# Loading the first two batches of b one by one, and entering the block through GpSimd, in a batched A^T B^T matmul

## The chip, the cores and the metric

The kernel runs on one core of a Trainium2 chip. The metric is device microseconds of one execution. The profile covers one execution; its span (123.0 us before) is about 2 us shorter than the time outside it (124.96 us).

## The reference

```python
batch, m, k, n = 16, 512, 512, 512
a: [batch, k, m] float32      b: [batch, n, k] float32
reference = np.matmul(a.transpose(0, 2, 1), b.transpose(0, 2, 1))   # [batch, m, n] float32
```

33.55 MB are read and 16.78 MB written, 50.33 MB in all. a is stored with k first and is used as it is; b is transposed on the chip.

## The kernel before

Every load and the last stores are issued by SP; the other stores by ScalarE. b comes in pairs of batches: a partition holds 8 rows of 2 KB, 16 KB that lie together in memory, and the loads move them in 16 KB packets. VectorE casts a pair to bf16 in two halves, TensorE transposes it through an identity (`turn`), VectorE copies the PSUM result to SBUF once for each batch, and TensorE multiplies (`half`). The pair is transposed as a whole: batch 0's copy can start only after both halves are transposed.

```python
b_v = b.rearrange("(p g) (ni r) k -> p (g ni) r k", g=2, r=NR)      # NR = 8
...
with tc.tile_critical():                       # entered through SP
    ...
    def run_sp(sp):
        for i in range(B):
            for p in ([0] if i == 0 else [(i + 1) // 2] if i % 2 and i + 1 < B else []):
                if p >= PAIRS:
                    sp.wait_ge(turned, p - PAIRS + 1)
                sp.dma_start(b_sb[p % PAIRS][:], b_v[p]).then_inc(b_in[p % PAIRS], 16)
            s, use = i % LOADS, i // LOADS     # LOADS = 4
            if use:
                sp.wait_ge(summed, MO * (i - LOADS) + 1)
            if i % 2 == 0 and i // 2 >= OUTS:
                sp.wait_ge(o_out[i // 2 % OUTS], 16 * (i // 2 // OUTS))
            sp.dma_start(a_sb[s][:], a_v[i]).then_inc(a_in[s], 16)
        ...                                    # the last three pairs of outputs are stored here
    def run_act(act):
        cast_a(act, 0)
        for i in range(B - 1):
            cast_a(act, i + 1)
            copy_out(act, i, slice(2, 4), oa_go)
            j, odd = divmod(i - LAG, 2)        # LAG = 3
            if odd and 0 <= j < H - TAIL:
                store(act, j)
        ...
```

## Time and profile before

| | before |
|---|---|
| time, median of the first 3 runs | 124.96 us (124.85 to 125.09) |
| span of the profiled execution | 123.0 us |
| DMA queues, share of the 16 engines' span | 77.2% + 20.1% |
| rate of the DMA engines from 6 to 118 us | 425 to 430 GB/s |
| TensorE, VectorE, ScalarE busy | 70%, 46%, 38% |

The packets of the two queues fill 97% of the 16 DMA engines' span. The lines behind the table, and what follows from them, are in the prediction.

### The profile page before, as it was taken

The numbers are of one execution on the slowest core, as the hardware profiler recorded it, in microseconds if no ns is written. First come the engines' busy times: TensorE is split into PE (matmuls) and PEld (weight loads), VectorE is DVE, ScalarE is ACT, GpSimd is POOL, SyncE is SP. The second block draws the span as 40 slices with busy tenths as digits, with TensorE's granted clock in tenths as the row PEclk, the third lists the DMA queues.
The fourth block names the chain that finished last, engine by engine and source line by source line (L and its number), as shares of the span: only waits on it lengthen the run. The fifth ranks groups of instructions, "written<-read, shape, count | busy, mean of one in ns | idle before, by whom it ended". The sixth has DMA issues, their size and how long they took to land. (4 is left out here: it accounts for less than half of the span.)

```text
span 123.0 us, 1086 instructions
## 1 busy us (share of the span) xinstructions
PE 86.1 (70%) x400; PEld 49.7 (40%) x400; DVE 56.4 (46%) x48; ACT 46.8 (38%) x34; POOL 0.7 (1%) x6
## 2 busy tenths in 40 slices
PE   0006497997999799779930799965992679979600
PEld 0006344642755464346410546442640526437300
DVE  0016368478295755917039107780719306171200
ACT  4003209537717903176300950329230490750300
POOL 2000000000000000000000000000000000000000
PEclk9999999999999999999995557999999558999995
DMA  4999999999999999999999999999999999999992
GB/s 91 394 400 458 400 424 456 429 394 456 426 397 448 434 376 432 426 440 440 416 421 429 458 408 418 429 426 437 453 397 432 426 426 426 429 426 426 429 424 115
DMA packets 5648, 50.33 MB, mean 409 GB/s; under 512 B 528, under 2 KB 528, under 8 KB 528
## 3 DMA queue, kind: packets, MB, share of 16 engines
q1 hardware_dynamic: 4288, 39.85, 77.2%
q10 hardware_dynamic: 1360, 10.49, 20.1%
HBM read 33.55 MB, written 16.78 MB: 409 GB/s over the span
## 5 line engine op out<-in xcount | busy, mean ns | idle before, releaser
L219 PE MATMUL o_ps<-bt_sb,a_bf 128*128 128x512 bf16 x256 | 65.1, 403 | 7.1 <-PEq L194 6.6
L135 ACT CAST a_bf<-a_sb 128x2048 bf16<-128x2048 f32 x16 | 30.4, 1900 | 40.8 <-DMA a_sb<-in_a_dram 40.8
L219 PEld LDWEIGHTS o_ps<-bt_sb,a_bf 128*128 128x128 bf16 x256 | 28.5, 115 | 37.5 <-issue 15.0
L205 PE MATMUL bt_ps<-identity,b_bf 128*128 128x128 f32 x144 | 24.3, 323 | 22.7 <-PEq L194 22.7
L144 DVE COPY o_sb<-o_ps 128x1024 f32<-128x1024 f32 x16 | 19.6, 1224 | 35.8 <-PE o_ps L219 35.8
L205 PEld LDWEIGHTS bt_ps<-identity,b_bf 128*128 128x128 f32 x144 | 22.2, 212 | 28.2 <-issue 27.2
L152 DVE CAST b_bf<-b_sb 128x2048 bf16<-128x2048 f32 x16 | 19.5, 1221 | 19.1 <-DMA b_sb<-in_b_dram 19.1
L144 ACT COPY o_sb<-o_ps 128x1024 f32<-128x1024 f32 (+1 forms) x17 | 16.4, 962 | 28.0 <-PE o_ps L219 28.0
L161 DVE COPY bt_sb<-bt_ps 128x1024 f32<-128x1024 f32 x16 | 19.5, 1216 | 3.1 <-PE bt_ps L205 3.1
L135 ACT ACT_TABLE_LOAD x1 | 1.3, 1283 | 0.9 <-SPq L51 0.9
L122 POOL TENSOR_SCALAR_AFFINE_SELECT identity<-identity 128x128 f32<-128x128 f32 x1 | 0.3, 294 | 0.2 <-POOL identity L120 0.2
L120 POOL MEMSET identity<- 128x128 f32 x1 | 0.2, 205 | 0.7 <-SPq L51 0.7
L265 POOL MEMSET const-bfloat16-1.0<- 128x1 bf16 x1 | 0.1, 102 | 0.0
L265 POOL MEMSET const-uint8-127<- 128x1 uint8 x1 | 0.1, 102 | 0.0
L265 POOL MEMSET const-float32-0.0<- 128x1 f32 x1 | 0.1, 99 | 0.2 <-issue 0.2
L265 POOL MEMSET const-float32-1.0<- 128x1 f32 x1 | 0.1, 99 | 0.0
## 6 DMA issues: line engine op xcount, KB each, us to landing
b_sb<-in_b_dram SPq DMA_DIRECT2D x8, 2048.0 KB, 20.4
a_sb<-in_a_dram SPq DMA_DIRECT2D x16, 1024.0 KB, 17.5
out_dram<-o_sb ACTq DMA_DIRECT2D x5, 2048.0 KB, 15.2
out_dram<-o_sb SPq DMA_DIRECT2D x2, 2048.0 KB, 13.6
out_dram<-o_sb SPq DMA_DIRECT2D x2, 1024.0 KB, 6.3
```

What stands on the lines that cost most here:

```text
L120: pool.memset(identity[:], 0.0).then_inc(id_go, 1)
L122: pool.affine_select(out=identity[:], in_=identity[:], compare_op=mybir.AluOpType.not_equal, fill=1.0, base=0, pattern=[[-1, P]], channel_ ...
L135: act.copy(a_bf[i % 2][:], a_sb[s][:]).then_inc(ac_go, 1)
L144: copy(o_sb[i // 2 % OUTS][:, i % 2, rm, :], o_ps[h][:, p, :]).then_inc(go, 1)
L152: dve.tensor_copy(b_bf[:, r, :], b_sb[p % PAIRS][:, r, :]).then_inc(bc_go, n)
L161: dve.tensor_copy(bt_sb[g][:].rearrange("p j (ni r) -> p j ni r", r=NR), bt_ps[:].rearrange("p j r (g ni) -> p g j ni r", g=2)[:, g],).the ...
L205: last = pe.transpose(bt_ps[:, j, r, :], w[:, r, j, :], identity[:])
L219: last = pe.matmul(o_ps[h][:, q, :], a_r[:, rk, 2 * h + q, :], bt_h[:, rk // 2, rk % 2, :], start=(rk == 0), stop=(rk == KO - 1),)
L265: nc = _bacc.Bacc("TRN2", target_bir_lowering=False, num_devices=1)
```

## The change

The intent is an earlier start of computing. The first pair of b is loaded as two single batches, each in 8 KB packets, so that batch 0 can be cast and transposed while batch 1 is on its way; its PSUM copy no longer waits for batch 1. Later pairs stay as they were. The entry of the block is coordinated by GpSimd instead of SP, so that SP can issue sooner.

```diff
+    b0_v = b[0:2].rearrange("g (ni no) k -> g ni no k", no=NR // 2)
-    with tc.tile_critical():
+    with tc.tile_critical(sync_engine=nc.gpsimd.engine):
         def run_sp(sp):
+            for g in range(2):
+                sp.dma_start(
+                    b_sb[0][:, g * NR // 2:(g + 1) * NR // 2, :], b0_v[g]
+                ).then_inc((b_first, b_in[0])[g], 16)
             for i in range(B):
-                for p in ([0] if i == 0 else [(i + 1) // 2] if i % 2 and i + 1 < B else []):
+                for p in [(i + 1) // 2] if i % 2 and i + 1 < B else []:
... in run_dve, cast_b(0, 0) waits for b_first; turn(0, 0) waits for turned_first and copies in two parts:
+                if p == 0:
+                    r = NR // 2
+                    bt = bt_ps[:, :, g * r:(g + 1) * r, :].rearrange("p j r ni -> p j ni r")
... in run_pe, the first half's transposes are announced by themselves:
-                if h:
-                    last.then_inc(turned, 1)
+                if h or first:
+                    last.then_inc(turned if h else turned_first, 1)
```

## The prediction

> **What bounds the kernel now.** I read the page's slices first, then the rate in small stretches, then the waits, then the two ends of the timeline. The slices settle most of it:
>
> ```profile
> PE   0006497997999799779930799965992679979600
> DMA  4999999999999999999999999999999999999992
> DMA packets 5648, 50.33 MB, mean 409 GB/s; under 512 B 528, under 2 KB 528, under 8 KB 528
> ```
>
> The DMA row is 9 in every slice but the first and the last. No compute engine is like that: TensorE has idle slices until the end, and ScalarE and VectorE are each busy less than half of the span. The rate in stretches (columns: stretch, its length, busy time of PE, PEld, DVE, ACT, POOL, granted clock, DMA share, GB/s) says how full "9" is:
>
> ```profile
> 1.50:2.00 0.50, 0.00 (x0) 0.00 (x0) 0.00 (x0) 0.50 (x1) 0.29 (x1) 1.00 0.54 131
> 2.00:2.50 0.50, 0.00 (x0) 0.00 (x0) 0.00 (x0) 0.18 (x1) 0.00 (x0) 1.00 1.47 262
> 2.50:3.00 0.50, 0.00 (x0) 0.00 (x0) 0.00 (x0) 0.00 (x0) 0.00 (x0) 1.00 0.65 164
> 3.00:3.50 0.50, 0.00 (x0) 0.00 (x0) 0.00 (x0) 0.00 (x0) 0.00 (x0) 1.00 0.46 131
> ...
> 6.00:30.00 24.00, 17.00 (x80) 10.55 (x80) 13.78 (x12) 9.01 (x6) 0.00 (x0) 1.00 1.01 428
> 30.00:60.00 30.00, 26.37 (x134) 15.57 (x135) 17.91 (x16) 15.60 (x12) 0.00 (x0) 1.00 1.01 425
> 60.00:90.00 30.00, 21.86 (x96) 12.18 (x93) 14.15 (x12) 10.96 (x8) 0.00 (x0) 0.83 1.01 430
> 90.00:118.00 28.00, 20.89 (x94) 11.43 (x92) 10.56 (x9) 9.93 (x9) 0.00 (x0) 0.88 1.00 425
> 118.00:120.50 2.50, 0.00 (x0) 0.00 (x0) 0.00 (x0) 0.00 (x0) 0.00 (x0) 0.79 1.01 426
> 120.50:121.00 0.50, 0.00 (x0) 0.00 (x0) 0.00 (x0) 0.00 (x0) 0.00 (x0) 0.50 0.40 164
> ```
>
> From 6 to 120.5 us the 16 engines move 425 to 430 GB/s with a share of 1.0, in the stretch that only reads (6 to 30) as in the one that only writes (118 to 120.5). There is no hole in which a faster compute chain would let a transfer start sooner. The span can therefore be written as a sum along the DMA engines. The packet records in the trace (not a view of the page) give 309 ns (median) for an 8 KB packet and 611 ns for a 16 KB one. An engine carries a sixteenth of the 2048 a packets and the 2048 out packets of 8 KB, and of the 1024 b packets of 16 KB: 256 x 0.309 + 64 x 0.611 = 79.1 + 39.1 = 118.2 us; its 33 small semaphore packets of 9 ns add 0.3. In front stand 0.95 us until the first load is issued and 1.0 us until its first packet starts (1.96). The first packets are slow, 0.9 to 1.9 us instead of 0.61; summed over those that start before 3.4 us and divided by 16 this costs about 0.75 us. That makes 1.96 + 118.5 + 0.75 = 121.2; the last packet ends at 121.45, on one engine that lags the others. Its landing is seen at 121.93, and the waiting for `stored` and the closing barrier make 123.0. The timed median of 124.96 has about 2 us more than the span, outside the profile (the profiled execution itself took 124.78). So some 118.5 us of 125 are bytes, and what a change that leaves the bytes alone can touch is the 6.5 us at the ends.
>
> The waits (who waited <- for whom: total us, times, longest us) look as if there were more to win:
>
> ```profile
> ACT a_bf L135 <- DMA a_sb<-in_a_dram: 40.8, 9, 9.1
> DVE o_sb L144 <- PE o_ps L219: 35.8, 14, 6.3
> DVE b_bf L152 <- DMA b_sb<-in_b_dram: 19.1, 6, 8.8
> PE bt_ps L205 <- PEq L194: 22.7, 9, 10.2
> ```
>
> The compute engines wait for loads, and the longest wait of VectorE, 8.8 us, is the one at the start that the change attacks. But these are waits of engines that are not the bound. The beginning of the timeline (start us, duration us) has the chain that the change shortens, and the end has what follows the last load:
>
> ```profile
> 8.81 2.36 DVE L152 CAST b_bf<-b_sb 128x2048 bf16<-128x2048 f32 x2 [8.81 <-DMA b_sb<-in_b_dram]
> 10.18 3.61 PE L205 MATMUL bt_ps<-identity,b_bf 128*128 128x128 f32 x16 [10.18 <-PEq L194]
> 11.25 1.90 ACT L135 CAST a_bf<-a_sb 128x2048 bf16<-128x2048 f32 x1 [9.06 <-DMA a_sb<-in_a_dram]
> 13.83 1.23 DVE L161 COPY bt_sb<-bt_ps 128x1024 f32<-128x1024 f32 x1 [2.66 <-PE bt_ps L205]
> 15.55 3.80 PE L219 MATMUL o_ps<-bt_sb,a_bf 128*128 128x512 bf16 x16 [1.76 <-PEq L194]
> ...
> 92.23 24.65 SPq L86 DMA_DIRECT2D out_dram<-o_sb x4
> ```
>
> The last store is issued until 116.88, starting about 116.54. Its 1.05 MB are the last that move. At 426 GB/s they need 2.46 us, and they end about 120.8, so they start about 118.3; with the 1.0 us from issue to first packet seen at the start they could have started at 117.5. The compute tail therefore has a margin of some 0.8 us (estimate from these numbers): finishing earlier gains nothing, finishing more than 0.8 us later would open a hole.
>
> **What the Trainium skill says.** "DMA: Bandwidth & Descriptors", section "Bandwidth", gives 425 GB/s for a 16 MB load and 435 as the fabric ceiling of the 16 engines; the trace agrees with 425 to 430. The same page, "Issuing engines are not separate DMA queues", says that DMAs share the same 16 engines whoever starts them, and that issuing elsewhere saves sequencer time only; here two queues with 77.2% and 20.1% of the engines' span add to 97%, so the trace agrees. "TensorE: Matmul & The Clock Gate", "Part 1: The HAM clock gate", says that TensorE is clocked at half until it has been busy for some microseconds, and again after an idle window, and that the phase of that window varies. The trace has the clock at 0.5 in two stretches (about 65 to 75 and 96 to 102 us). That is the one thing that could move the tail.
>
> **The change part by part.**
>
> *Entry through GpSimd.* The gathering instruction at the entry of the critical block moves from SP to GpSimd. In the trace SP leaves the opening barrier at 0.67, runs its NOP at 0.72, passes its own semaphore at 0.80 and issues at 0.95. Now SP waits for a semaphore from GpSimd, which released the opening barrier itself at 0.61 and whose instructions there follow each other every 0.08 us: its NOP would be at about 0.69, SP would pass about 0.72 to 0.75. Gain on the path: some 0.05 us. At the exit the block's gathering also moves to GpSimd, but SP sits 4.6 us waiting for the last store there; nothing.
>
> *The first pair in two loads.* Same 2.10 MB, now 256 packets of 8 KB instead of 128 of 16 KB: per engine 16 x 309 = 4.94 us for 8 x 611 = 4.89, +0.06 us with one more semaphore packet, all on the DMA path. One more issue on SP of about 0.43 us moves every later issue back by that, but the first load keeps the engines busy for 2.5 us, so none of it shows. The slow first packets: if the slowness is a time, nothing changes; if it is a cost per packet, smaller packets change it by a few tenths either way. I take 0 with 0.3 of doubt.
>
> *Compute start.* Batch 0 of b lands about 2.5 us sooner (half the bytes at 427 GB/s): near 6.2 instead of 8.8. Its cast ends at 7.5, its 8 transposes at 9.3, while the second half lands at 8.8, is cast until 10.0 and turned until about 11.9. The PSUM copy, now in two parts of some 0.62 us (estimate: half of 1.23), runs 10.0 to 11.3 instead of 13.83 to 15.06. Then a0 becomes what the first matmul waits for: it lands at 11.2 as before, because it follows the same bytes in the queue, and its cast ends at 13.2. The first matmul thus starts near 13.2 instead of 15.55: 2.3 us sooner. This gain does not reach the end. The cast of a3 at 28.51 waited for its landing, so at batch 3 the gain falls to some 1.3 us, and a cast near 97 us again waited 6.6 us for a load whose issue depends on earlier stores landing. All of that is scheduling inside a DMA stream that is full anyway.
>
> Sum: 124.96 - 0.05 + 0.06 + 0 = about 124.95; I put 124.9.
>
> **The rivals.** (1) The earlier start is kept to the end and the time falls by up to 2.3 us, to 122.7. For it: the first matmul really moves, and waits of 40.8 and 19.1 us for loads look large. Against it: the DMA share is 1.0 from 3.5 to 120.5 us, so 50.33 MB would have to move at 436 GB/s, which no long stretch shows. I give it 1 in 100 for 2%. (2) The start-up of the DMA engines is what changes: smaller first packets fill the engines sooner and recover part of the 0.75 us, time about 124.3; or 8 KB packets each pay the slow start and the time is about 125.3. The low rate between 2.5 and 3.5 us speaks for something to win; that no packet record says why it is low, against. (3) The tail comes out of step: since compute runs 1 to 2 us ahead, stores enter the engines earlier and the last loads land a little later in the stream, or the half-clock stretch falls on the last batches. The slow stretch before 102 us had 8 matmuls in 3.48 us where 1.83 is usual, so 1.65 us; less the 0.8 of margin this costs about 1 us, 126. For it: the margin is thin. Against it: compute is ahead, not behind.
>
> **Range and chances.** Sources of doubt: start-up 0.3 us, the lagging engine at the end 0.3, run-to-run spread 0.1, the tail 1 us at a chance of 1 in 8, upward only. That gives 124.2 to 125.7. For 2% the time would have to fall to 122.5, or rise to 127.5; the first needs more than all that stands outside the bytes and the fixed ends, the second a hole of 2.5 us. Faster 1%, within 97%, slower 2%.
>
> **What would show it.** Right: the DMA share stays at 1.0 and 425 to 430 GB/s from about 4 to 120 us; the first cast of b begins near 6.2 and the first matmul near 13.2, its last wait being the cast of a; the first issue on SP is at about 0.90; the span is 122.6 to 123.6. Wrong: a stretch before 120 us with a share well under 1 (the tail); a sum of the first 3.5 us that differs clearly from 0.34 MB (the start-up); or a steady rate other than 427, which I take to be fixed and on which the whole prediction rests.

## The result, and the profile after

125.08 us (median of 6 runs, 124.92 to 125.30) against 124.97 for the kernel before in the same rounds (6 runs). The ratio is 1.0013, 95% interval 1.0000 to 1.0027: the same within 2%. Ratios here and below are the mean time of one kernel's runs over that of the other's of the same rounds, so they are not quite the ratio of the medians.

The slices of the changed kernel's page:

```profile
DMA  3999999999999999999999999999999999999992
DMA packets 5792, 50.33 MB, mean 409 GB/s; under 512 B 544, under 2 KB 544, under 8 KB 544
```

Its compute waits (total us, times, longest us):

```profile
ACT a_bf L143 <- DMA a_sb<-in_a_dram: 39.2, 9, 8.5
DVE o_sb L152 <- PE o_ps L239: 38.9, 13, 6.4
DVE b_bf L163 <- DMA b_sb<-in_b_dram: 19.3, 8, 5.8
PE bt_ps L225 <- PEq L214: 17.4, 10, 7.1
```

The DMA row is full from the second slice to the last but one, as before. VectorE's longest wait for b fell from 8.8 to 5.8 us, which is the head start the change wanted, and yet its total wait for b is 19.3 us where it was 19.1: what is not waited for at the start is waited for later.

The beginning of the changed kernel's timeline (start us, duration us):

```profile
0.89 0.86 SPq L97 DMA_DIRECT2D b_sb<-in_b_dram  x2
...
5.75 1.23 DVE L163 CAST b_bf<-b_sb 128x2048 bf16<-128x2048 f32 x1 [5.75 <-DMA b_sb<-in_b_dram]
...
10.70 1.90 ACT L143 CAST a_bf<-a_sb 128x2048 bf16<-128x2048 f32 x1 [8.53 <-DMA a_sb<-in_a_dram]
...
12.94 5.12 PE L239 MATMUL o_ps<-bt_sb,a_bf 128*128 128x512 bf16 x16 [1.39 <-PEq L214]
```

SP issues at 0.89 instead of 0.95; the first cast of b starts at 5.75 instead of 8.81; the first matmul at 12.94 instead of 15.55, held only by the cast of a0. But its 16 matmuls take 5.12 us where the same 16 took 3.80, so 2.6 us of head start are 1.3 by the end of batch 0 (18.06 against 19.35).

For the rate, the same stretches of both kernels (columns as in the prediction; the last two are DMA share and GB/s; a packet counts where it starts). Before:

```profile
3.00:6.00 3.00, 0.00 (x0) 0.00 (x0) 0.00 (x0) 0.00 (x0) 0.00 (x0) 1.00 0.88 360
42.00:46.00 4.00, 4.00 (x25) 2.72 (x24) 1.78 (x3) 1.28 (x1) 0.00 (x0) 1.00 0.97 397
118.00:118.50 0.50, 0.00 (x0) 0.00 (x0) 0.00 (x0) 0.00 (x0) 0.00 (x0) 1.00 1.02 426
```

After:

```profile
3.00:6.00 3.00, 0.00 (x0) 0.00 (x0) 0.25 (x1) 0.00 (x0) 0.00 (x0) 1.00 1.03 431
42.00:46.00 4.00, 4.00 (x23) 2.44 (x21) 2.36 (x2) 0.45 (x1) 0.00 (x0) 1.00 1.00 373
118.00:118.50 0.50, 0.00 (x0) 0.00 (x0) 0.00 (x0) 0.00 (x0) 0.00 (x0) 1.00 0.94 393
```

These lines show where the gain goes. The changed kernel is at full rate from 3 us, where the kernel before is at 360 GB/s. Between 42 and 46 us it loses: the share stays at 1.00 while the rate falls to 373 GB/s, so the engines are not idle; their packets take longer. (All of the slow ones are loads; the store packets take their steady 309 ns.) At 118 us there is a small hole.

Counted from the trace's packet records (each packet's bytes spread over its duration), this is how far the stream had come, in MB:

| by | before | after | after minus before |
|---|---|---|---|
| 6 us | 1.253 | 1.384 | +0.131 (0.31 us at 427 GB/s) |
| 42 us | 16.630 | 16.743 | +0.113 |
| 48 us | 19.133 | 19.105 | -0.028 |
| 116 us | 48.249 | 48.229 | -0.020 |

The change puts the stream 0.3 us ahead, keeps that for 36 us, and gives all of it back within 6 us, when the first stores enter (first store packet at 44.04 us before, 43.23 after). Two measures of slow packets are used from here on. *Start cost* is the sum, over the packets that start before 5 us, of duration less the steady duration of that packet size (611 ns for 16 KB, 309 for 8 KB, 159 for 4 KB), divided by 16: us per engine. *First-store cost* is the same for 40 to 50 us.

| | start cost | first-store cost |
|---|---|---|
| before | 0.80 | 0.18 |
| after | 0.57 | 0.51 |

The start cost differs from one execution to the next: in after, shift_half, shift_all and shift_ports, whose first 25 us are the same program, it is 0.57, 0.30, 0.63 and 0.32. Their position at 6 us is steadier (1.370 to 1.384 MB; 1.230 to 1.280 in the four traces that start with a 16 KB load of b), so the gain is better read from that.

### The profile page after: what moved, and what is told of

The parts are those of the page before. It is cut to its first block, busy times and chain, and to the rows that moved or that the text cites. A ratio compares the mean times of both kernels' runs of the same rounds, so it can differ in the third digit from the quotient of the medians.

```text
span 123.1 us, 1090 instructions
## 1 busy us (share of the span) xinstructions
PE 89.7 (73%) x400; PEld 49.7 (40%) x400; DVE 56.6 (46%) x49; ACT 46.7 (38%) x34; POOL 0.7 (1%) x6
## 5 line engine op out<-in xcount | busy, mean ns | idle before, releaser
L239 PE MATMUL o_ps<-bt_sb,a_bf 128*128 128x512 bf16 x256 | 69.2, 422 | 9.7 <-PEq L214 9.2
L239 PEld LDWEIGHTS o_ps<-bt_sb,a_bf 128*128 128x128 bf16 x256 | 29.2, 118 | 42.9 <-issue 22.7
L225 PEld LDWEIGHTS bt_ps<-identity,b_bf 128*128 128x128 f32 x144 | 21.5, 211 | 23.7 <-issue 22.9
L163 DVE CAST b_bf<-b_sb 128x2048 bf16<-128x2048 f32 x16 | 19.6, 1223 | 19.3 <-DMA b_sb<-in_b_dram 19.3
L181 DVE COPY bt_sb<-bt_ps 128x1024 f32<-128x1024 f32 (+1 forms) x17 | 19.5, 1153 | 0.5 <-PE bt_ps L225 0.5
```

The source lines that it names most:

```text
L163: dve.tensor_copy(b_bf[:, r, :], b_sb[p % PAIRS][:, r, :]).then_inc(bc_go, n)
L181: done = dve.tensor_copy(bt_sb[g][:, j].rearrange("p j (ni r) -> p j ni r", r=r), bt[:, j])
L225: last = pe.transpose(bt_ps[:, j, r, :], w[:, r, j, :], identity[:])
L239: last = pe.matmul(o_ps[h][:, q, :], a_r[:, rk, 2 * h + q, :], bt_h[:, rk // 2, rk % 2, :], start=(rk == 0), stop=(rk == KO - 1),)
```

## The experiments

Twelve kernels were run. The theory at the outset was that the stream gains at its start through the form of the first loads, and that this gain is lost at the first stores. The rivals were that the entry makes the gain, that the loss is chance, and that the loss comes from the head start in compute.

### entry_only: the kernel before with the GpSimd entry

```diff
-    with tc.tile_critical():
+    with tc.tile_critical(sync_engine=nc.gpsimd.engine):
```

> The kernel before with the GpSimd entry alone. My theory (the change wins about 0.3 us at the start of the DMA stream through its first loads and gives it back where the first stores enter, 42 to 46 us; the entry itself is worth 0.06): first issue on SP at 0.885 instead of 0.949 us, first packets as slow as before (about 0.26 MB moved by 3.5 us), time 0.05 to 0.1 us below the kernel before, which lies inside the noise: ratio 0.999 to 1.000. Rival (the entry carries all of the start gain): about 0.32 MB by 3.5 us and the stream 0.3 us ahead at 6 us.

124.95 us against 124.84; ratio 1.0014 (0.9997 to 1.0030). First issue at 0.89 us, first packet at 1.92 instead of 1.96, 0.28 MB by 3.5 us; at 6 us the stream leads by 0.019 MB, 0.04 us. The entry is worth what the trace of before let one work out, and no more; the lead of 0.31 us is not its doing. The time, which should have been 0.05 us less, shows nothing at this resolution.

### split_only: the change without the GpSimd entry

```diff
-    with tc.tile_critical(sync_engine=nc.gpsimd.engine):
+    with tc.tile_critical():
```

> The changed kernel with the entry through SP as before. My theory: the stream is ahead of the kernel before by about 0.25 us at 6 us (the 0.31 of the changed kernel less 0.06 for the entry), the first stores cost 0.3 to 0.5 us per engine in slow packets at 42 to 46 us, time 1.000 to 1.002 of the kernel before. Rival (no gain at the start from the smaller packets): the stream is not ahead at 6 us. Rival (the loss at the first stores is chance): it can come out anywhere from 0.15 to 0.5 us per engine, and the time with it.

125.06 against 124.84; ratio 1.0012 (0.9994 to 1.0029). Lead of 0.083 MB, 0.19 us, at 6 us; start cost 0.47; first-store cost 0.45. Both the loss and most of the gain come without the entry, so they belong to the loads.

### held: the change with the first cast of b held back, to take away its head start

```diff
                 if p == 0 and h == 0:
                     dve.wait_ge(b_first, 16)
+                    dve.wait_ge(b_in[0], 16)
```

> The changed kernel, but the first cast of b waits for both first loads, so that the compute head start goes and the DMA start stays. My theory: lead of 0.3 us at 6 us as in the changed kernel; the first store is issued near 40.2 us instead of 39.6, fewer 16 KB packets of b are then under way, the slow packets at 42 to 46 us cost near 0.16 us per engine as before, and the time is 0.2 to 0.3 us below the changed kernel: ratio to the kernel before 0.997 to 0.999. Rival (chance): ratio as the changed kernel's, 1.000 to 1.003, with any loss at the first stores.

125.11 against 124.84; ratio 1.0023 (1.0006 to 1.0040). The first cast of b moved from 5.75 back to 8.28 us, and the time stayed the changed kernel's (1.0023 and 1.0013, intervals overlapping). But the head start of the matmuls was hardly taken away. The lines of held, and of a_first further below, beside 12.94 in the changed kernel and 15.55 before:

```profile
13.43 4.27 PE L240 MATMUL o_ps<-bt_sb,a_bf 128*128 128x512 bf16 x16
```

```profile
17.47 3.80 PE L221 MATMUL o_ps<-bt_sb,a_bf 128*128 128x512 bf16 x16 [1.76 <-PEq L196]
```

The first matmul, which waits for a0 in any case, moved by 0.5 us only, so held shows that the early cast is worth nothing measurable, and not more. a_first makes the better test: its first matmul comes 1.9 us later than before and 4.5 later than in the changed kernel, and its time is none the longer (0.9989). My expectation was wrong in its middle: the first store was issued at 39.62 us, exactly as in the changed kernel, because what comes before it is the cast of a5, which waits for its landing (37.84 us in the changed kernel, 37.81 in held), and not the start. So held could not separate what I meant it to; its first-store cost is 0.50. Its stretch at the first stores (the stretches view of held):

```profile
42.00:46.00 4.00, 4.00 (x23) 2.45 (x21) 2.35 (x2) 0.43 (x1) 0.00 (x0) 1.00 1.01 377
```

Again a share of 1.0 at 377 GB/s: the same slow packets, without the early cast.

### late_store: all stores of ScalarE two batches later

```diff
-    LAG = 3
+    LAG = 5
```

> The changed kernel with the stores held back by two batches (LAG 5 instead of 3): the first store is issued near 52 us, when other loads are under way. My theory in its narrow form (the loss comes because the first stores meet the 16 KB packets of b's fifth pair): the slow packets at 42 to 46 us vanish, and the first stores, later, meet 8 KB packets of a and cost at most 0.2 us per engine; time 0.2 to 0.3 us below the changed kernel if the tail holds. In its wide form (the first stores cost something wherever they enter): 0.2 to 0.5 us per engine at about 55 us. Rival (something at 42 to 46 us that has nothing to do with stores): slow packets stay at 42 to 46 us.

129.34 against 124.84: 1.0355 (1.0337 to 1.0373), a clear miss. The slow packets did leave 42 to 46 us (0.10 us per engine from 40 to 50) and came at the new place of the first store, 0.28 from 50 to 55. But more followed: packets slow by up to 0.39 us turn up near 67, 83, 86, 97 and 104 us, 0.3 to 1.0 us per engine in each of the worst 5 us. Over the whole run slow packets add 3.4 us per engine to those of the changed kernel, of the 4.5 us by which the last packet ended later; most of the rest is holes. With stores held back, loads wait for stores to land (SP waited 46.5 us for them, 33.5 in the changed kernel), and the stream alternates between long stretches of one kind. The stretches view of late_store:

```profile
60.00:90.00 30.00, 22.40 (x100) 11.58 (x98) 13.82 (x13) 11.25 (x8) 0.00 (x0) 0.89 1.00 402
90.00:118.00 28.00, 19.35 (x80) 10.26 (x80) 8.56 (x8) 9.71 (x8) 0.00 (x0) 0.82 0.97 382
```

Share near 1, rate 402 and 382 where the kernel before has 430 and 425. So the narrow form is refuted, and in this run the first stores cost something at their new place too. It is not a cost of every such change: in the other 13 traces stores rejoin a stream of pure loads two or three times more (near 55, 71 and 86 us, after 1.4 to 4.9 us without a store), and the slow packets around each of these sum to 0.01 us per engine at most. Only the first stores cost there; why late_store pays again and again is not shown.

### nudge_late and nudge_early: the first store alone moved

In the changed kernel the first store goes behind the next cast; in the kernel before it goes ahead of the copy it otherwise follows.

```diff
                 cast_a(act, i + 1)
+                if i == 5:            # nudge_early, on the kernel before: i == 4
+                    store(act, 0)
                 copy_out(act, i, slice(2, 4), oa_go)
                 j, odd = divmod(i - LAG, 2)
-                if odd and 0 <= j < H - TAIL:
+                if odd and 0 < j < H - TAIL:
```

> The changed kernel with its first store alone issued one cast later (near 40.6 us instead of 39.6, as late in its stream as in the kernel before). Theory A (what the first store costs depends on when it meets the loads of b's fifth pair): slow packets at 40 to 47 us cost at most 0.2 us per engine instead of 0.44 to 0.50, the start lead of 0.3 us lives on, time 0.2 to 0.3 us below the changed kernel, ratio to the kernel before 0.997 to 0.999. Theory B (the split start leaves the 16 engines in step, their landings 0.4 us apart instead of 1.1, and engines in step meet the first store harder): 0.4 to 0.5 us stay, ratio 1.000 to 1.002.

> The kernel before with its first store alone issued ahead of the copy it otherwise follows (near 38.7 us instead of 40.5). Theory A: the first store now meets more of the 16 KB packets of b's fifth pair, the slow packets cost 0.4 us per engine or more instead of 0.05 to 0.16, ratio to the kernel before 1.002 to 1.003. Theory B: the engines are still out of step, cost 0.2 or less, ratio 0.999 to 1.001.

nudge_late: the store was issued at 40.32 us (only 0.7 later, but its first packet came at 43.86, near the 44.04 of before); first-store cost 0.37; 124.99 against 124.93, ratio 1.0011 (0.9991 to 1.0031). nudge_early: issued at 38.45, first packet at 42.02, cost 0.15; 124.96, ratio 1.0006 (0.9986 to 1.0025). In the main the cost stayed with the kernel and did not follow the store. Theory A, the meeting with b's fifth pair, is refuted in the early direction: 65 of its 16 KB packets start within 4 us of the first store packet, 30 in the changed kernel, and yet the cost is 0.15 instead of 0.4 or more. In the late direction it can be a part: 0.37 is above the 0.2 that it foresaw, but below the 0.45 to 0.51 of split_only, held and the changed kernel.

### quarter: batch 0 in 4 KB packets

```diff
+            for r in range(0, NR // 2, 2):
+                sp.dma_start(b_sb[0][:, r:r + 2, :], b0_v[0][:, r:r + 2, :]).then_inc(b_first, 16)
+            sp.dma_start(b_sb[0][:, NR // 2:NR, :], b0_v[1]).then_inc(b_in[0], 16)
```

> The changed kernel with batch 0 of b in two loads of 512 KB with 4 KB packets. If the slow start is a cost of each engine's first packets that grows with their size, the excess over the steady packet time before 5 us falls from 0.47 to 0.57 us per engine to 0.3 or less, and 6 us sees 0.05 MB more than the 1.38 MB of the changed kernel by then. If it is a fixed time, excess and lead stay within 0.1 us of the changed kernel's. The total stays within 0.2 us of the changed kernel's, because the first stores cost 0.4 to 0.5 as there.

125.07 against 124.93; ratio 1.0008 (0.9991 to 1.0025). Start cost 0.65, another 0.18 from 5 to 10 us, and only 1.191 MB by 6 us: behind the kernel before, not ahead of the changed one. Both of my forms failed. Smaller is not simply better at the start; 8 KB was better than 16 and than 4 here, and no run says why. First-store cost 0.33.

### a_first: the kernel before with a0 ahead of b

```diff
+            sp.dma_start(a_sb[0][:], a_v[0]).then_inc(a_in[0], 16)
             for i in range(B):
                 ...
-                sp.dma_start(a_sb[s][:], a_v[i]).then_inc(a_in[s], 16)
+                if i:
+                    sp.dma_start(a_sb[s][:], a_v[i]).then_inc(a_in[s], 16)
```

> The kernel before with a0 loaded ahead of the first pair of b: the stream starts with 8 KB packets and nothing else of the change is there. My theory (the size of the first packets makes the lead): about 0.2 to 0.3 us ahead of the kernel before at 6 us, excess before 5 us near 0.5 us per engine instead of 0.8 to 0.9, engines in step (landings of the first load of b within 0.5 us). At the first stores theory A says nothing sure, since compute starts as before but the stream is ahead; theory B says 0.4 to 0.5 us of slow packets, and a time of 1.000 to 1.002 of the kernel before. Rival for the start (the lead came from the two loads, not from the packet size): no lead.

124.82 against 124.93; ratio 0.9989 (0.9971 to 1.0006), the lowest of all and still the same. Start cost 0.47, lead of 0.083 MB (0.19 us) at 6 us: as split_only, without any split. Starting with 8 KB packets is enough for the gain. The first store came later (issued 42.36, first packet 46.06), met mostly 8 KB packets of a, and cost 0.62. So the loss, too, comes without the split, without separate transposing, without b's 16 KB packets and without any head start in compute (first matmul at 17.47 us). One thing here speaks against the first store packets as its cause: 0.21 of the 0.62 lies in loads that ended before the first store packet began (0 to 0.05 in the other traces). No record shows what goes on between the issue of the store, at 42.36, and that packet.

### shift_half, shift_all and before_again: are the engines in step?

The landings of one load are 1.1 us apart over the 16 engines in the kernel before, 0.4 in the changed one, 0.3 in a_first. The measure R in the expectation says how much the engines' packets start together: 1 when all start at the same point of their period, near 0 when they are spread over it. An extra 8 KB packet on half of the engines should put them out of step.

```diff
                 sp.dma_start(a_sb[s][:], a_v[i]).then_inc(a_in[s], 16)
+                if i == 3:                               # shift_all: 0:16
+                    sp.dma_start(o_sb[4][0:8, 0, :, :], a_v[0][0:8]).then_inc(extra, 16)
```

(ScalarE and VectorE wait for `extra` ahead of batch 8, which first writes that buffer.)

> The changed kernel plus one extra load, behind a3, of 8 partitions of 8 KB into a buffer not yet in use: one more 8 KB packet on 8 of the 16 engines, which puts them half a 16 KB packet (0.309 us) behind the others. Measure of step: R, the concentration of the start times of 16 KB packets within their period of 0.611 us, taken from 3.5 to 1.8 us before the first store packet (0 evenly spread, 1 all together). In the ten traces so far R is 0.06 to 0.25 where the first stores cost 0.06 to 0.19 us per engine in slow packets (40 to 50 us), and 0.40 to 0.82 where they cost 0.28 to 0.62. Theory B (engines in step pay more when the first stores come): R falls to 0.3 or less and the cost to 0.2 or less; the time stays near the changed kernel's or 0.1 to 0.2 us below, because the 8 engines carry 0.31 us more. Rival (the step and the cost only have a common origin in the start with 8 KB packets): R falls, the cost stays at 0.35 or more, and the time rises by up to 0.3 us.

> The control: the same extra load over 16 partitions, one more 8 KB packet on each engine, so that all shift alike. Theory B: R stays at 0.4 or more, the cost at 0.35 to 0.55 us per engine, and the time is 0.3 us (one packet of 0.309) above the changed kernel: ratio to the kernel before 1.003 to 1.005. Rival (the extra load itself or its place calms the first stores): cost 0.2 or less.

> The kernel before once more, for a second profile. Theory B: R at 0.3 or less and a cost of 0.2 us per engine or less at the first stores, excess before 5 us of 0.8 to 0.9. If R or cost come out like the changed kernel's (0.4 or more), the split between the two families is chance, and the loss at the first stores explains nothing of the change.

shift_half 126.31 against 124.72 (1.0116, 1.0097 to 1.0135); shift_all 126.34 (1.0128, 1.0112 to 1.0143). Both failed as tests: the extra load of 64 or 128 KB itself slowed its neighbours: the slow packets from 25 to 30 us sum to 1.2 us per engine, 0.07 in the changed kernel. The stretches view, shift_half and then the changed kernel, in the same 5 us:

```profile
25.00:30.00 5.00, 4.12 (x18) 1.74 (x16) 3.81 (x4) 2.16 (x2) 0.00 (x0) 1.00 1.02 324
```

```profile
25.00:30.00 5.00, 4.04 (x18) 1.84 (x18) 3.96 (x4) 3.06 (x3) 0.00 (x0) 1.00 1.06 444
```

Share 1.02, 324 GB/s. After that the first stores cost 0.04 in both, with R at 0.33 and 0.22 (from only 23 and 20 packets): the control, meant to stay in step, did not. This agrees with theory B but agrees also with any theory in which a disturbance at 28 us spares one at 44.

before_again (one run, 124.6 us; state unknown, being single) came out as expected: R 0.17, start cost 0.73, first-store cost 0.09. Together with the rest this speaks against chance: the four traces that start with 16 KB packets have first-store costs of 0.06 to 0.18, the six undisturbed ones that start with 8 KB packets and keep the place of their stores within about 3 us have 0.37 to 0.62.

### shift_ports: the same shift without its side effect, and the last store in two parts

```diff
-                    sp.dma_start(o_sb[4][0:8, 0, :, :], a_v[0][0:8]).then_inc(extra, 16)
+                    sp.dma_start(o_sb[4][0:32:4, 0, :, :], a_v[0][0:8]).then_inc(extra, 16)
...
-            sp.wait_ge(last_go, 3)
-            store(sp, H - 1, slice(1, 2))
+            for mo, go, n in ((slice(0, 2), dve_last, 1), (slice(2, 4), last_go, 2)):
+                sp.wait_ge(go, n)
+                sp.dma_start(out_v[B - 1][:, mo, :], o_sb[(H - 1) % OUTS][:, 1, mo, :]).then_inc(stored, 16)
```

> shift_half again without what spoiled it: there the extra load itself cost 1.24 us per engine at 27 to 29 us. Its 8 rows went to partitions 0 to 7; now they go to partitions 0, 4, ... 28, which by the page on DMA of the Trainium skill (its descriptor swizzle) are the partitions of eight different engines in an ordinary load. Also in this kernel, and separable by time since it acts after 113 us: the last store is cut in two halves, the first issued when VectorE has copied its part. Theory B: the extra load costs little (below 0.3 us per engine at 25 to 30 us), R falls to 0.3 or less at 43 us, the first stores cost 0.2 us per engine or less instead of 0.44 to 0.50, and the stream still leads the kernel before by 0.1 us or more at 50 us; time within 0.2 us of the kernel before. Rival: R falls and the first stores cost 0.35 or more; time 0.3 us above the changed kernel. If R stays at 0.4 or more with a cost of 0.28 or more, B is neither helped nor harmed. The cut store: no stretch of half a microsecond between 117 and 120 us below 400 GB/s by packet overlap.

125.56 against 124.88; ratio 1.0068 (1.0048 to 1.0089), slower than I expected. The extra load cost nothing this time: the slow packets from 25 to 30 us sum to 0.07 us per engine, as in the changed kernel (0.08). R came out at 0.46 and the first-store cost at 0.47.

R has a badly chosen window: it lies before the first store packet, wherever that is, and in nudge_early, shift_half and shift_all it held mostly 8 KB packets, for which a period of 611 ns says little. (The R given here is over the 16 KB packets alone, as the expectation defines it. A first count took in every packet of the window, and had 0.06, 0.11, 0.07 and, for shift_ports, 0.33.) R' in the table is the same concentration over one load that all kernels have in common, b's fourth pair (16 KB packets between 30 and 38.5 us, those within 1.5 us of their median start, 76 to 80 of them). By R' shift_ports is at 0.51 and the changed kernel at 0.54: one packet more on half of the engines, undisturbed, did not put them out of step (the landings of one load spread from 0.44 to 0.69 us, no more). So this run is of the kind that by my own wording neither helps nor harms B.

As for the rest of this kernel, the hole at 118 us was closed (427 GB/s from 118.0 to 118.5 by packet overlap, 396 in the changed kernel), yet the last packet ended at 121.81 instead of 121.43: half of the engines carry 0.31 us more, and the 4 KB packets of the cut store (159 ns each, so 318 for 8 KB) add 0.07. These 0.38 us do not account for all of the time: by the ratios (1.0068 and 1.0013) the kernel is some 0.7 us slower than the changed one, and the rest is not explained.

All traces together, sorted by R':

| kernel | first packets | R' | R | first-store cost |
|---|---|---|---|---|
| entry_only | 16 KB | 0.11 | 0.12 | 0.06 |
| before_again | 16 KB | 0.11 | 0.17 | 0.09 |
| nudge_early | 16 KB | 0.19 | 0.16 | 0.15 |
| shift_half | 8 KB | 0.20 | 0.33 | 0.04 |
| shift_all | 8 KB | 0.31 | 0.22 | 0.04 |
| before | 16 KB | 0.38 | 0.25 | 0.18 |
| quarter | 4 KB | 0.40 | 0.44 | 0.33 |
| shift_ports | 8 KB | 0.51 | 0.46 | 0.47 |
| split_only | 8 KB | 0.52 | 0.46 | 0.45 |
| after | 8 KB | 0.54 | 0.40 | 0.51 |
| a_first | 8 KB | 0.63 | 0.63 | 0.62 |
| held | 8 KB | 0.65 | 0.60 | 0.50 |
| nudge_late | 8 KB | 0.76 | 0.73 | 0.37 |
| late_store (50 to 55 us) | 8 KB | 0.83 | 0.82 | 0.28 |

Apart from the two disturbed runs, the cost rises with R' up to a_first; nudge_late and late_store at the end, which fall off, are the two of the 8 KB family whose store was moved to a later place. That makes step a lead, and a correlation found afterwards in 14 traces, by a measure chosen afterwards: no run changed the step and left all else alone. The spread of the landings of one load, from which the idea came, does not sort the costs: before 40 us it is 0.55 us in entry_only (cost 0.06) and 0.52 in split_only (0.45), 1.1 in before (0.18) and in quarter (0.33). The cause of the loss is open.

## Why the prediction was right

**The bound: right, and it decided everything.** The stream of bytes sets the time. In the changed kernel it ran at 427 and 428 GB/s by packet overlap from 6 to 30 and from 60 to 116 us, and the last packet ended at 121.43 us where it had ended at 121.45.

**The entry: right.** Predicted 0.05 us; the issue moved by 0.064 and the first packet by 0.057 us.

**The first pair in two loads: the size was off, and the sign.** I put +0.06 us for the packets and 0 for the slow start with 0.3 of doubt. The start cost fell by 0.23 us. This is the first half of rival 2, which I had priced at 124.3 us; it came true, as split_only and a_first show, and still the time did not move, because of a step I did not have.

**The step I did not have: the first stores.** I took the steady rate to be fixed and named it as what the whole prediction rests on. It is not fixed between 42 and 46 us: 397 GB/s before (share 0.97), 373 after (share 1.00). The trace of the kernel before could have told: its 397 lies inside the stretch from 30 to 60 us, which was read as one number, 425. A second sign of being wrong that I had named came too: the first 3.5 us carried 0.40 MB (115 GB/s) instead of 0.34. The first-store cost rose by 0.33 us (0.18 to 0.51), which is the lead of 0.31 us lost. That this loss goes with the start of the stream, and not with the entry, the split, the head start or (in the main) the time of the store, is shown by entry_only, by a_first (for the split and the head start) and by the two nudges, with one profiled execution of each. What in the start causes it stays open; engines in step are one lead. Two errors of about 0.3 us with opposite signs thus cancelled in my sum.

**Compute start: right in direction and nearly in size.** First cast predicted near 6.2 us, measured 5.75; first matmul 13.2 against 12.94. At the cast of a3, where I put 1.3 us, 0.55 were left (27.96 against 28.51). I did not foresee that half of the gain would go at once: the 16 matmuls of batch 0 took 5.12 us instead of 3.80. "TensorE: Matmul & The Clock Gate", Part 1, says that the clock is released only after some microseconds of sustained work. In the trace's clock records the first release is at 15.8 us in the changed kernel (13.6 before), so its first seven matmuls fall ahead of it and took 0.55 to 0.63 us each, the others 0.39. The same holds in all 14 traces, and what is left of the head start depends on when the release comes: with it at 18.8 us, split_only finished batch 0 at 19.54, no earlier than the kernels without the change (19.07 to 19.42), and held, whose first cast comes 2.5 us later, had it at 14.5 and finished first of all, at 17.70. No run set the time of the release by itself. That none of the head start reaches the end is best shown by a_first: it finished batch 0 at 21.26 us, 3.2 later than the changed kernel, and its ratio of 0.9989 is the lowest here.

**The tail: the margin right, the direction not.** The margin was estimated at 0.8 us, and I counted on compute being ahead at the end. In the changed kernel the last store was issued 0.91 us later than before (117.45 against 116.54), and a hole just opened: 396 GB/s by overlap from 118.0 to 118.5 us, worth 0.03 us per engine. In before_again it was issued at 117.67 and the hole was deeper:

```profile
118.00:118.50 0.50, 0.00 (x0) 0.00 (x0) 0.00 (x0) 0.00 (x0) 0.00 (x0) 1.00 0.21 82
```

That is the unchanged kernel, so the tail's margin comes and goes from run to run. I had named the half-clock stretch of TensorE as the one thing that could move the tail, and the traces agree: in the nine that keep the order of loads and late stores and have no extra load, the later the last such stretch before 110 us ends, the later the last store is issued, from 102.0 us (nudge_late, issued at 116.31) over 102.4 (before, 116.54) and 104.5 (after, 117.45) to 105.2 (before_again, 117.67). No run varied the clock alone. A stream that runs a few tenths ahead could lose part of them here next; no run shows that.

No version beat both kernels; a_first came nearest, and its interval includes 1.

## What to carry to other kernels

When the DMA engines are busy all along, write the time as packets times their measured durations plus the two ends, and ask of a change which of these terms it touches; a compute engine's wait of 9 us at the start can be shortened by 3 and the time stays where it was. Read the DMA share together with GB/s: a share of 1 with a lower rate means slow packets, which no idle-time view shows. A gain at one place of a full stream is not banked until the stream's position, in MB, is compared at several later times.

## What the Trainium skill lacked or had wrong

- "DMA: Bandwidth & Descriptors", "Bandwidth": it has the steady rate right (425 GB/s there, 425 to 430 here), but no slow start: the first packets cost 0.3 to 0.9 us per engine beyond their steady duration in the traces here.
- The same page has nothing on what a change between loads and stores costs: 0.04 to 0.62 us per engine when the first stores join a stream of loads, at most 0.01 when stores rejoin loads near 55, 71 and 86 us in the same runs, and up to 1.0 us per engine in 5 us in late_store, which alternates (3.5% slower in all).
- The same page, "Latency and other measured facts", gives about 600 ns to the first byte for this path, but not from where it is counted. Here the first packet started 1.01 us after the issue on SP began (0.949 to 1.956) and 0.62 us after that instruction of 0.386 us ended; the figure fits the second.
- The same page, "The descriptor swizzle", gives the partitions that each engine writes, but not what a small load off that pattern costs the loads around it: with 8 or 16 rows of 8 KB into partitions 0 to 7 or 0 to 15, the slow packets from 25 to 30 us summed to 1.2 us per engine; with 8 rows into partitions 0, 4, ... 28 to 0.07, as without an extra load. The mapping itself was not measured.
